# Recurrent branch of a two-layer hybrid block: preparation, solve and chunk chain laid out anew, TensorE in program order inside the branch

## The chip, the cores and the metric

One core of a Trainium2 chip runs the whole program: two layers of a diffusion-transformer block on one sequence, the second layer with a mixture of experts. The metric is the device time of one execution in microseconds. Before the change three executions took 2982.87, 2986.39 and 2990.86 us; the median is 2986.39 us.

## What is computed

Each layer projects the normalised tokens (256 context tokens and 256 tokens of the sequence, 512 together) into the inputs of three branches: latent attention, neighbourhood attention and a recurrent branch in the manner of RWKV-7. The branches are gated, merged and added to the tokens, and a feed-forward part follows, dense in layer 0, with experts in layer 1. Only the recurrent branch matters here. Its reference is a scan over tokens with a 64x64 state per head, 8 heads, once forward and once backward, over the context first and then over the sequence:

```
def step(S, inp):
    r_t, w_t, k_t, v_t, kk_t, a_t = inp
    sa = jnp.einsum('bhij,bhj->bhi', S, -kk_t)
    S = S * w_t[:, :, None, :] + sa[..., None] * (kk_t * a_t)[:, :, None, :] + v_t[..., None] * k_t[:, :, None, :]
    return S, jnp.einsum('bhij,bhj->bhi', S, r_t)
```

Before the scan, `kk` is the key times a gain, normalised to length 1 per head; the decay is w = exp(-exp(w_log)), with w_log from a low-rank projection of tanh; `a` is a sigmoid of a low-rank projection; the direction's key is k(1 + (a - 1) k_a). After it the two directions are added, normalised per head, a bonus (the sum over a head of r, the keys and a gain, times v) is added, and the whole is gated.

## The kernel before

**Layout.** The projections are computed transposed: a tile is 128 channels by 512 tokens. Four such tiles hold the 512 channels of r, k and v each. The branch takes them in two halves (f = 0 and 1) of two tiles, that is four heads; `rw_half` (L587) does one half, in these stages.

**Front** (`rw_front`, L551). For both tiles: kk times its gain, its square on ScalarE, the sum of squares per head by a matmul with a 0/1 matrix (L562), square root, maximum and reciprocal on 64 x 512 elements (L565 to L568), a matmul that spreads the result over each head's channels (L572), and the product. Then v is transposed (L581). In the first half the front runs first; in the second it is a generator that the chain of the first half advances step by step, from its fourth step on.

**Preparation** (L600 to L665). For each tile i and direction d: two low-rank matmuls (L609, L614), two tanh on ScalarE, an affine line (L618), a scan that sums the logarithms of the decay within chunks of 64 tokens (L620), for the backward direction two lines that turn the sum around (L622, L623), the exponentials P and iP (L626, L627), the decay over a whole chunk PC (L632), and the scaled operands: KR from kk and r (L635 to L641), BK from iP, a, and the direction's key (L644 to L653). Temporaries share one tag with five buffers (L548). At the end of each tile i stands the bonus: a VectorE line (L660), a matmul with a block matrix (L662) and the product with v (L664).

**Solve and merge.** Small pair matmuls inside the chunks (L684, L686), masked by VectorE (L689); VectorE transposes (L697), solves triangular systems of 16 x 16 in 14 steps of two lines (L703, L705) and transposes back (L709, L710). TensorE then builds the inverses of 32 and of 64 from them with 32 x 32 matmuls: L719, L735 and L739, L763 and L764, L771 and L772, with copies between them by VectorE and ScalarE.

**Chain** (L876 to L912). Eight steps, each of which takes one chunk forward and one backward. A step multiplies the old state with KR (L882), copies the right side (ScalarE, L885), applies the inverse (L892), copies the result (VectorE L894, ScalarE L895), adds to the state (L847, then the product with the decay on VectorE, L850) and writes outputs (L858, L865). The next step's inner products, masks, transposed keys and right side are computed in between (`inner`, `mask`, `keys`, `right`).

**Output** (`rw_out`, L918). Mean and variance per head on VectorE, transposes (L938), gain, bonus, gate (L943) and the store.

**What sets the order.** The program's text gives every engine an order of priority; the planner of the framework then lists the instructions of each engine, and takes an instruction of lower priority first where by its cost model the earlier one isn't ready. The rest of TensorE's work in this stage is the filler: `serve` (L451) yields the input projections tile by tile, each in 8 steps of three matmuls (a weight is split into a high and a low part, L314 to L316; ScalarE makes the high part, L469, and GpSimd the low part, L470), and after each tile it advances the modulation of a later stage (L339). `weave` (L1634) runs the stages' generators and draws filler from `serve`, as much as their yields ask for, in microseconds of TensorE time; a table of numbers per layer gives the yields (L1691):

```
K.W = (dict(prep=5.517, solve=1.0, merge=2.541, chain=1.41, front=1.212, mod=0.976), ...)[l]
weave(rwkv(l, t0), K.srv, False)
```

There is a yield behind each preparation (L658), several in the solve (L696 to L711), two in front of L735 and L763, two in the merge and three in each step of the chain. What is left of the filler goes to the attention that follows (L1700). In layer 1 the tiles which are needed for the sequence alone have 256 columns. `need` (L497) draws filler until a given tile is there; `shift` (L503) makes the branch's inputs of a finished tile, one line on ScalarE and two on VectorE. PSUM has five banks for the branch, two for the projections and one for the modulation.

Of the kernel before, what the change touches and what calls it, by code (L numbers as in the profile page):

```python
# [14 lines left out]
AF = mybir.ActivationFunctionType  # L15
OP = mybir.AluOpType
# [8 lines left out]
DEC = math.exp(-0.5)  # L25
# [160 lines left out]
class Kern:  # L186
# [346 lines left out]
    def rw_common(s, l):  # L533
        nc = s.nc
        s.rw_derived(l)
        s.share()
        for tag, n in (("z", 6), ("kk", 2), ("lora", 1), ("kds", 1)):
            s.t([128, T], tag, n)
        s.g2 = s.t([128, 512], "g2", 1)
        nc.sync.dma_start(s.g2, s.I["lora"][l, :, 2])  # L540
        s.m16 = s.t([128, 96], "m16", 1)
        nc.sync.dma_start(s.m16, s.I["cst"][:, KCST:])
        s.wd = s.need("wd")
        nc.scalar.activation(s.wd, s.wd, AF.Tanh)
        s.ad = s.need("ad")
# [5 lines left out]
    def rw_front(s, l, f, t0y):  # L551

        V, A, PE = s.nc.vector, s.nc.scalar, s.nc.tensor
# [3 lines left out]
        for i in range(2):  # L557
            q = s.t([128, T], "kk", 2)
            V.tensor_scalar(q, k[i], s.col(l, "kk", 2 * f + i), None, op0=OP.mult)
            sq = s.tmp()  # L560
            A.activation(sq, q, AF.Square)
            PE.matmul(st[32 * i:32 * i + 32], s.c("hs")[:, 2:], sq, start=True, stop=True)  # L562
            kk.append(q)
        rt = s.tmp()
        A.activation(rt[:64], st[:64], AF.Sqrt)  # L565
        yield 1.0
        V.tensor_scalar(rt[:64], rt[:64], 1e-12, None, op0=OP.max)
        V.reciprocal(rt[:64], rt[:64])  # L568
        yield 3.0
        for i in range(2):  # L570
            p = s.ps(tag="rw")
            PE.matmul(p, s.c("hst", 128)[32 * i:32 * i + 32], rt[32 * i:32 * i + 32], start=True, stop=True)  # L572
            V.tensor_tensor(kk[i], kk[i], p, OP.mult)
# [13 lines left out]
    def rw_half(s, l, f, t0y):  # L587
# [14 lines left out]
        for i in range(2):  # L602
            hp = 2 * f + i
            kd0 = None
            for d in range(2):
# [12 lines left out]
                V.tensor_scalar(lw, lw, -0.5 * DEC, -0.5 * DEC, op0=OP.mult, op1=OP.add)  # L618
                cum = s.tmp()
                V.tensor_tensor_scan(cum, s.c("scanm"), lw, 0.0, OP.mult, OP.add)  # L620
                if d:
                    V.tensor_tensor(lw, lw, cum, OP.subtract)  # L622
                    V.tensor_tensor(c8(lw), c8(lw), c8(cum)[:, :, 63:64].to_broadcast([128, 8, 64]), OP.add)  # L623
                    cum = lw
                P, iP = s.tmp(), s.tmp()
                A.activation(P, cum, AF.Exp)  # L626
                A.activation(iP, cum, AF.Exp, scale=-1.0)  # L627
                P8, q8 = c8(P), c8(kk[i])
                e = 0 if d else 63
                for a in (0, 4):  # L630
                    P4 = P8[:, a:a + 4, e:e + 1]
                    V.tensor_tensor(PC[:, a:a + 4, i, d], (P4[:, ::-1] if d else P4).to_broadcast([128, 4, 2]),  # L632
                                    s.c("hs")[:, 2:4].unsqueeze(1).to_broadcast([128, 4, 2]), OP.mult)
# [9 lines left out]
                u = s.tmp()  # L643
# [5 lines left out]
                kd = s.t([128, T], "kds", 1) if not d else s.tmp()  # L649
                V.tensor_scalar(kd, ta, s.kc2[l][:, hp:hp + 1], s.kc1[l][:, hp:hp + 1], op0=OP.mult, op1=OP.add)  # L650
                V.tensor_tensor(kd, kd, k[i], OP.mult)
# [7 lines left out]
            u = s.tmp()  # L659
            V.scalar_tensor_tensor(u[:, t0y:], kd0[:, t0y:], s.col(l, "rk", hp), r[i][:, t0y:], op0=OP.mult, op1=OP.mult)  # L660
            pb = s.ps(tag="rw")
            PE.matmul(pb[:, t0y:], s.c("bd"), u[:, t0y:], start=True, stop=True)  # L662
            bn = s.t([128, T], "bonus", 2)
            V.tensor_tensor(bn[:, t0y:], pb[:, t0y:], v[i][:, t0y:], OP.mult)  # L664
# [46 lines left out]
        yield s.W["solve"] * 4.0  # L711
# [11 lines left out]
        yield s.W["solve"] * 2.0  # L723
# [31 lines left out]
        yield s.W["solve"] * 3.0  # L755

        W = s.piece(2, 2048, 32, 32)
        for j in range(2):
            p = s.ps(tag="rw")
# [6 lines left out]
            V.tensor_copy(W[64:96, 16 * j:16 * j + 16, :].rearrange("p a b -> p (a b)"), p[64:96])  # L766
            p = s.ps(tag="rw")
# [5 lines left out]
            yield s.W["merge"]  # L773
# [93 lines left out]
        st = {}  # L867
# [8 lines left out]
        for n in range(8):  # L876
# [12 lines left out]
            yield s.W["chain"]  # L889
# [6 lines left out]
            yield s.W["chain"]  # L896
            if not last:
                mask(n + 1, 0, nx)
                Hn = end(n, H, st)
                mask(n + 1, 1, nx)  # L900
                values(n + 1, nx)
            if out:
                outputs(n, H, st)
            if not last:
                keys(n + 1, nx)
                right(n + 1, nx)
                H, st = Hn, nx
            yield s.W["chain"]
# [9 lines left out]
    def rw_out(s, l, f, R, t0):  # L918
# [14 lines left out]
        V.tensor_tensor(y, y, st[:, 2, :g].unsqueeze(2).to_broadcast([128, g, 64]), OP.mult)  # L933
        for i in range(2):
# [711 lines left out]
def body(tc, I, O, dbg=None, marks=None):  # L1646
    with ExitStack() as ctx:
# [9 lines left out]
        def rwkv(l, t0):  # L1657
            K.rw_common(l)
            for f in range(2):
# [4 lines left out]
                K.rw_out(l, f, K.R, t0)  # L1664
                yield 1.0

        for l in range(2):
            t0 = 256 * l
            with K.phase(f"o{l}", True, mm=2, md=1):
# [20 lines left out]
                with K.phase(f"rw{l}", rw=5):  # L1690
                    K.W = (dict(prep=5.517, solve=1.0, merge=2.541, chain=1.41, front=1.212, mod=0.976), dict(prep=4.665, solve=1.0, merge=2.178, chain=1.56, front=1.173, mod=0.666))[l]  # L1691
                    weave(rwkv(l, t0), K.srv, False)
# [62 lines left out]
```

## Time and profile before

| what | value |
|---|---|
| median of three runs | 2986.39 us |
| the profiled execution's own time | 2989.12 us |
| its span in the profile | 2987.4 us |
| mean granted clock of TensorE | 0.957 of full |
| busy: TensorE, VectorE, ScalarE, GpSimd | 2815.1, 1901.3, 1621.5, 369.9 us |
| HBM read and written | 554.38 and 24.64 MB |

A row of the waits says which instruction waited for which, in total, how often and the longest. Lines are those of the kernel above; `prw` is a PSUM bank of the branch, `pmm` one of the projections. "issue" is time in which the engine waited for nothing that the profile shows. In a view by stretches each engine's busy time is followed by the number of its instructions in brackets; the granted clock is a share of full speed, whose two levels are 1.0 (2.4 GHz) and 0.5 (1.2 GHz). A matmul on f32 data appears as several records.

### The profile page before, as it was taken

How to read it: one execution, taken by the hardware profiler on the slowest of the kernel's cores; microseconds unless marked ns; L12 is line 12 of the kernel's file. 1: busy time of each engine (PE TensorE's matmuls, PEld its weight loads, DVE VectorE, ACT ScalarE, POOL GpSimd, SP SyncE). 2: the span in 40 equal slices, each digit the busy share in tenths (PEclk: the TensorE clock that was granted, in tenths of full speed). 3: DMA queues.
4: the chain of work that ended last, by engine and by line, in shares of the span. 5: the costliest groups of instructions: out<-in, count | busy, mean ns of one | idle time of the engine just before them, and what ended most of it. 6: DMA issues, size and time to landing. Idle time of an engine off the chain costs nothing. (4 is left out here: it accounts for less than half of the span.)

```text
span 2987.4 us, 48726 instructions
## 1 busy us (share of the span) xinstructions
PE 2815.1 (94%) x19774; PEld 2168.4 (73%) x19774; DVE 1901.3 (64%) x2654; ACT 1621.5 (54%) x2449; POOL 369.9 (12%) x287
## 2 busy tenths in 40 slices
PE   7989979999999999997997979989999999999998
PEld 3566667676777888765766856778878787887876
DVE  4653662527754333267347256779988988888897
ACT  3423423447644332253343436667877777777776
POOL 3221221220010000133233400010000000000000
PEclk9989979999999999998997988989999999999999
DMA  7433311441432333343342333669989999998995
GB/s 273 160 130 103 131 57 61 158 143 57 128 127 80 97 99 104 117 143 110 103 149 95 108 104 109 193 239 361 359 320 363 353 350 342 356 361 335 362 352 205
DMA packets 109016, 582.26 MB, mean 195 GB/s; under 512 B 12912, under 2 KB 26608, under 8 KB 86896
## 3 DMA queue, kind: packets, MB, share of 16 engines
q1 hardware_dynamic: 94640, 557.57, 52.1%
q10 hardware_dynamic: 13632, 19.93, 1.8%
q8 instruction: 157, 2.57, 0.4%
q0 software_dynamic: 512, 1.57, 0.1%
q14 instruction: 75, 0.61, 0.1%
HBM read 554.38 MB, written 24.64 MB: 194 GB/s over the span
## 5 line engine op out<-in xcount | busy, mean ns | idle before, releaser
L314 PE MATMUL pmm<-big,whi 128*128 128x512 f32 (+2 forms) x1392 | 534.4, 385 | 11.1 <-ACT stage L958 3.2
L315 PE MATMUL pmm<-big,whi 128*128 128x512 f32 (+2 forms) x1392 | 517.4, 372 | 7.3 <-DVE big L436 3.6
L316 PE MATMUL pmm<-big,wlo 128*128 128x512 f32 (+2 forms) x1392 | 515.9, 371 | 1.9 <-POOL wlo L470 1.9
L1552 DVE TENSOR_TENSOR mwlo<-share,mwhi 128x1024 fp32r<-128x1024 f32 x398 | 472.2, 1229 | 21.0 <-ACT mwhi L1551 11.7
L1551 ACT ACTIVATE mwhi<-share 128x1024 fp32r<-128x1024 f32 x404 | 423.8, 1059 | 94.2 <-PE pmm L316 68.2
L470 POOL TENSOR_TENSOR wlo<-wraw,whi 128x512 fp32r<-128x512 f32 (+1 forms) x228 | 305.0, 1341 | 721.5 <-ACT whi L469 691.9
L315 PE MATMUL pmm<-mwlo,big 128*128 128x512 f32 x896 | 355.1, 396 | 7.2 <-DVE mwlo L1552 6.7
L314 PEld LDWEIGHTS pmm<-big,whi 128*128 128x128 f32 (+1 forms) x1392 | 267.4, 192 | 117.5 <-issue 37.5
L314 PE MATMUL pmm<-mwhi,big 128*128 128x512 f32 x896 | 352.1, 393 | 0.6 <-ACT big L1439 0.6
L316 PE MATMUL pmm<-mwhi,big 128*128 128x512 f32 x896 | 349.8, 390 | 0.0
L299 DVE TENSOR_TENSOR wlo<-wraw,whi 128x512 fp32r<-128x512 f32 x236 | 158.7, 674 | 252.1 <-ACT whi L298 245.6
L1552 DVE TENSOR_TENSOR mwlo<-mraw,mwhi 128x1024 fp32r<-128x1024 f32 x264 | 310.9, 1223 | 9.1 <-ACT mwhi L1551 3.5
L1551 ACT ACTIVATE mwhi<-mraw 128x1024 fp32r<-128x1024 f32 x264 | 278.0, 1060 | 66.8 <-PE pmm L316 49.8
L315 PEld LDWEIGHTS pmm<-big,whi 128*128 128x128 f32 (+1 forms) x1392 | 267.9, 192 | 55.1 <-DVE big L436 6.0
L316 PEld LDWEIGHTS pmm<-big,wlo 128*128 128x128 f32 (+1 forms) x1392 | 268.1, 193 | 50.6 <-issue 5.1
L298 ACT ACTIVATE whi<-wraw 128x512 fp32r<-128x512 f32 x236 | 145.3, 617 | 288.4 <-PE pmm L315 271.9
L469 ACT ACTIVATE whi<-wraw 128x512 fp32r<-128x512 f32 (+1 forms) x228 | 141.8, 624 | 267.4 <-PE pmm L315 228.3
L315 PEld LDWEIGHTS pmm<-mwlo,big 128*128 128x128 f32 x896 | 168.3, 188 | 48.0 <-DVE mwlo L1552 12.3
L314 PEld LDWEIGHTS pmm<-mwhi,big 128*128 128x128 f32 x896 | 168.3, 188 | 36.3 <-ACT big L1439 1.3
L316 PEld LDWEIGHTS pmm<-mwhi,big 128*128 128x128 f32 x896 | 168.3, 188 | 33.4
L315 PE MATMUL pat<-mwlo,mhh 128*128 128x512 f32 x448 | 175.1, 391 | 1.6 <-DVE mwlo L1552 1.4
L314 PE MATMUL pat<-mwhi,mhh 128*128 128x512 f32 x448 | 174.4, 389 | 0.0
(407 smaller groups left out, 4487.0 us busy)
## 6 DMA issues: line engine op xcount, KB each, us to landing
share<-in_moe SPq DMA_DIRECT2D x100, 2048.0 KB, 9.4
mraw<-in_moe SPq DMA_DIRECT2D x66, 2048.0 KB, 9.5
wraw<-in_win SPq DMA_DIRECT2D x112, 512.0 KB, 3.5
wraw<-in_modw SPq DMA_DIRECT2D x80, 512.0 KB, 4.9
wraw<-in_ffn SPq DMA_DIRECT2D x60, 512.0 KB, 3.5
wraw<-in_wo SPq DMA_DIRECT2D x24, 512.0 KB, 3.8
wraw<-in_wout SPq DMA_DIRECT2D x16, 512.0 KB, 4.6
share<-in_modw SPq DMA_DIRECT2D x12, 512.0 KB, 9.0
```

Of the source, the lines that this page charges most:

```text
L298: nc.scalar.activation(hi, raw[:, a:a + b], AF.Copy)
L299: nc.vector.tensor_tensor(lo, raw[:, a:a + b], hi.bitcast(F32), OP.subtract)
L314: nc.tensor.matmul(out, a[0], b[0], start=first, stop=False)
L315: nc.tensor.matmul(out, a[0], b[1], start=False, stop=False)
L316: nc.tensor.matmul(out, a[1], b[0], start=False, stop=last)
L469: nc.scalar.activation(hi, raw[:, k:k + 4], AF.Copy)
L470: nc.gpsimd.tensor_tensor(lo, raw[:, k:k + 4], hi.bitcast(F32), OP.subtract)
L1551: nc.scalar.activation(hi, raw[:, a:a + 2], AF.Copy)
L1552: (nc.gpsimd if a in pool else nc.vector).tensor_tensor(lo, raw[:, a:a + 2], hi.bitcast(F32), OP.subtract)
```

## The change

- Front: the sums of squares come out with tokens on partitions (8 matmuls with 2 columns), so root, maximum and reciprocal work on 128 x 16 elements; 16 matmuls with a broadcast operand spread them again.
- Preparation: both affine lines go to ScalarE, where one takes its constant from a column added to `m16`; the backward scan runs over reversed views, and L622 and L623 fall away; P, u and the backward key reuse buffers; the forward PC is one line in place of two; the key's lines stand earlier.
- Bonus: VectorE's line writes into the bonus tile; matmul and product with v move into the chain's first two steps.
- Yields: solve 8 in place of 4 ahead of L719, none in front of L735 and L763, one in the merge, between its two first groups, one per chain step in place of three, one ahead of the output's transposes; new numbers in the table. In a chain step the masks and keys of the next step stand earlier.
- Order: the branch runs inside `manual_schedule` for TensorE, so TensorE's instructions of the branch, filler drawn in it included, are issued in program order. The other engines keep the planner's order.

```diff
@@ -538,8 +538,9 @@
-    s.m16 = s.t([128, 96], "m16", 1)
-    nc.sync.dma_start(s.m16, s.I["cst"][:, KCST:])
+    s.m16 = s.t([128, 97], "m16", 1)
+    nc.sync.dma_start(s.m16[:, 0:96], s.I["cst"][:, KCST:])
+    nc.vector.memset(s.m16[:, 96:97], -0.5 * DEC)
@@ -559,17 +561,23 @@
-        PE.matmul(st[32 * i:32 * i + 32], s.c("hs")[:, 2:], sq, start=True, stop=True)
+        for tt in range(4):
+            o = 8 * i + 2 * tt
+            PE.matmul(st[:, o:o + 2], sq[:, 128 * tt:128 * tt + 128], s.c("hs")[:, 2:4], start=(o == 0), stop=True,
+                      skip_group_check=True)
...
-    rt = s.tmp()
-    A.activation(rt[:64], st[:64], AF.Sqrt)
-    yield 1.0
-    V.tensor_scalar(rt[:64], rt[:64], 1e-12, None, op0=OP.max)
-    V.reciprocal(rt[:64], rt[:64])
-    yield 3.0
+    rt = s.t([128, 16], "rt", 2)
+    A.activation(rt, st[:, 0:16], AF.Sqrt)
+    V.tensor_scalar(rt, rt, 1e-12, None, op0=OP.max)
+    V.reciprocal(rt, rt)
+    yield 1.5
...
-        PE.matmul(p, s.c("hst", 128)[32 * i:32 * i + 32], rt[32 * i:32 * i + 32], start=True, stop=True)
+        for tt in range(4):
+            o = 8 * i + 2 * tt
+            for hh in range(2):
+                PE.matmul(p[64 * hh:64 * hh + 64, 128 * tt:128 * tt + 128], rt[:, o + hh:o + hh + 1].to_broadcast([128, 64]), s.id,
+                          start=(tt == 0), stop=True, skip_group_check=True)
@@ -615,22 +623,22 @@
-            V.tensor_scalar(lw, lw, -0.5 * DEC, -0.5 * DEC, op0=OP.mult, op1=OP.add)
+            A.activation(lw, lw, AF.Identity, bias=s.m16[:, 96:97], scale=-0.5 * DEC)
...
-            V.tensor_tensor_scan(cum, s.c("scanm"), lw, 0.0, OP.mult, OP.add)
-            if d:
-                V.tensor_tensor(lw, lw, cum, OP.subtract)
-                V.tensor_tensor(c8(lw), c8(lw), c8(cum)[:, :, 63:64].to_broadcast([128, 8, 64]), OP.add)
-                cum = lw
-            P, iP = s.tmp(), s.tmp()
+            rev = (lambda a: a[:, ::-1]) if d else (lambda a: a)
+            V.tensor_tensor_scan(rev(cum), s.c("scanm"), rev(lw), 0.0, OP.mult, OP.add)
+            P, iP = lw, s.tmp()
...
+            kd = s.t([128, T], "kds", 1) if not d else cum
+            A.activation(kd, ta, AF.Identity, bias=s.kc1[l][:, hp:hp + 1], scale=s.kc2[l][:, hp:hp + 1])
+            V.tensor_tensor(kd, kd, k[i], OP.mult)
...
-            for a in (0, 4):
-                P4 = P8[:, a:a + 4, e:e + 1]
-                V.tensor_tensor(PC[:, a:a + 4, i, d], (P4[:, ::-1] if d else P4).to_broadcast([128, 4, 2]),
-                                s.c("hs")[:, 2:4].unsqueeze(1).to_broadcast([128, 4, 2]), OP.mult)
+            for a, b in ((0, 4), (4, 8)) if d else ((0, 8),):
+                P4 = P8[:, a:b, e:e + 1]
+                V.tensor_tensor(PC[:, a:b, i, d], (P4[:, ::-1] if d else P4).to_broadcast([128, b - a, 2]),
+                                s.c("hs")[:, 2:4].unsqueeze(1).to_broadcast([128, b - a, 2]), OP.mult)
@@ -640,15 +648,12 @@
-            u = s.tmp()
+            u = P
...
-            kd = s.t([128, T], "kds", 1) if not d else s.tmp()
-            V.tensor_scalar(kd, ta, s.kc2[l][:, hp:hp + 1], s.kc1[l][:, hp:hp + 1], op0=OP.mult, op1=OP.add)
-            V.tensor_tensor(kd, kd, k[i], OP.mult)
@@ -656,12 +661,8 @@
-        u = s.tmp()
-        V.scalar_tensor_tensor(u[:, t0y:], kd0[:, t0y:], s.col(l, "rk", hp), r[i][:, t0y:], op0=OP.mult, op1=OP.mult)
-        pb = s.ps(tag="rw")
-        PE.matmul(pb[:, t0y:], s.c("bd"), u[:, t0y:], start=True, stop=True)
...
-        V.tensor_tensor(bn[:, t0y:], pb[:, t0y:], v[i][:, t0y:], OP.mult)
+        V.scalar_tensor_tensor(bn[:, t0y:], kd0[:, t0y:], s.col(l, "rk", hp), r[i][:, t0y:], op0=OP.mult, op1=OP.mult)
@@ -708,7 +709,7 @@
-    yield s.W["solve"] * 4.0
+    yield s.W["solve"] * 8.0
@@ -720,7 +721,6 @@
-    yield s.W["solve"] * 2.0
@@ -752,10 +752,11 @@
-    yield s.W["solve"] * 3.0
...
+        if j:
+            yield s.W["merge"]
@@ -764,13 +765,13 @@
+    for j in range(2):
...
-        yield s.W["merge"]
@@ -886,26 +887,30 @@
         if not last:
             inner(n + 1, nx)
         begin(n, H, st, out)
-        yield s.W["chain"]
+        if not last:
+            mask(n + 1, 0, nx)
         pu = [s.ps(tag="rw") for _ in range(2)]
         for i, hh, d, q in heads:
             PE.matmul(pu[d][bp(n, d), 64 * q:64 * q + 64], TT[HO[d], 16 * hh + 8 * i + ch[d], :], Rs[HO[d], 64 * q:64 * q + 64],
                       start=(q == 0), stop=(q == 3), skip_group_check=True)
         V.tensor_copy(st["uv"][0][bp(n, 0)].rearrange("p a b -> p (a b)"), pu[0][bp(n, 0), 0:256])
         A.activation(st["uv"][1][bp(n, 1)].rearrange("p a b -> p (a b)"), pu[1][bp(n, 1), 0:256], AF.Copy)
-        yield s.W["chain"]
         if not last:
-            mask(n + 1, 0, nx)
+            mask(n + 1, 1, nx)
+            keys(n + 1, nx)
+        yield s.W["chain"][f]
+        if not last:
             Hn = end(n, H, st)
-            mask(n + 1, 1, nx)
             values(n + 1, nx)
         if out:
             outputs(n, H, st)
         if not last:
-            keys(n + 1, nx)
             right(n + 1, nx)
             H, st = Hn, nx
-        yield s.W["chain"]
+        if n < 2:
+            pb = s.ps(tag="rw")
+            PE.matmul(pb[:, t0y:], s.c("bd"), bonus[n][:, t0y:], start=True, stop=True)
+            V.tensor_tensor(bonus[n][:, t0y:], pb[:, t0y:], v[n][:, t0y:], OP.mult)
         if n > 2:
             w = next(front, None)
             if w:
@@ -931,6 +936,7 @@
+    yield s.W["out"]
@@ -1661,8 +1667,7 @@
-            K.rw_out(l, f, K.R, t0)
-            yield 1.0
+            yield from K.rw_out(l, f, K.R, t0)
@@ -1688,8 +1693,10 @@
-                K.W = (dict(prep=5.517, solve=1.0, merge=2.541, chain=1.41, front=1.212, mod=0.976), dict(prep=4.665, solve=1.0, merge=2.178, chain=1.56, front=1.173, mod=0.666))[l]
-                weave(rwkv(l, t0), K.srv, False)
+                K.W = (dict(prep=5.5, solve=1.1, merge=1.9, chain=(1.9, 1.2), front=1.2, out=5.0, mod=0.976),
+                       dict(prep=4.7, solve=1.1, merge=1.9, chain=(1.9, 1.2), front=1.2, out=5.0, mod=0.666))[l]
+                with tc.manual_schedule(engines={mybir.EngineType.PE}):
+                    weave(rwkv(l, t0), K.srv, False)
```

## Rows read from the trace of the kernel before

**Rows 1.** Part 2 of the page: the span in 40 slices, in tenths.

```profile
PE   7989979999999999997997979989999999999998
...
PEclk9989979999999999998997988989999999999999
```

**Rows 2.** TensorE's waits, layer 0's recurrent branch: total us, times, longest us.

```profile
PE prw L662 <- DVE t L660: 16.2, 4, 6.7
PE prw L735 <- issue: 7.0, 4, 2.0
PE prw L719 <- DVE share L709: 6.8, 1, 6.8
```

**Rows 3.** TensorE's waits in the recurrent branch of layer 1.

```profile
PE prw L719 <- DVE share L709: 14.2, 2, 8.7
PE prw L662 <- DVE t L660: 12.9, 4, 4.2
PE prw L938 <- DVE share L933: 6.7, 2, 5.9
```

**Rows 4.** Stretches of layer 0: stretch, length, busy by engine, granted clock, DMA.

```profile
105.70:156.70 51.00, 44.58 (x170) 24.37 (x170) 39.45 (x59) 18.67 (x31) 12.43 (x9) 0.92 0.46 151
...
338.40:388.60 50.20, 40.33 (x149) 26.13 (x152) 42.67 (x61) 19.20 (x33) 16.03 (x12) 0.89 0.27 95
...
395.30:416.90 21.60, 14.83 (x62) 11.87 (x61) 20.40 (x33) 5.00 (x9) 6.70 (x5) 0.90 0.30 97
416.90:448.10 31.20, 25.84 (x928) 21.47 (x928) 9.85 (x13) 7.41 (x13) 4.44 (x4) 0.70 0.05 18
448.10:534.00 85.90, 85.90 (x949) 64.55 (x949) 21.41 (x39) 30.41 (x64) 16.35 (x13) 1.00 0.24 83
```

**Rows 5.** The same view, three stretches of layer 1.

```profile
1326.20:1370.60 44.40, 37.98 (x172) 23.54 (x171) 37.98 (x57) 19.77 (x34) 18.15 (x12) 0.96 0.51 164
...
1544.20:1592.50 48.30, 38.85 (x188) 26.21 (x187) 41.46 (x61) 19.77 (x35) 20.49 (x14) 0.86 0.42 143
...
1599.10:1623.00 23.90, 15.21 (x117) 15.01 (x119) 22.66 (x33) 7.92 (x16) 12.12 (x9) 0.79 0.37 116
```

**Rows 6.** VectorE by line, layer 0, second half: xcount, busy us, mean ns, idle before.

```profile
L651 DVE TENSOR_TENSOR t<-t,z 128x512 f32<-128x512 f32 x2 | 3.5, 1757 | 0.0
L618 DVE TENSOR_SCALAR t<-t 128x512 f32<-128x512 f32 x4 | 2.8, 694 | 2.0 <-ACT t L612 2.0
...
L664 DVE TENSOR_TENSOR bonus<-prw,z 128x512 f32<-128x512 f32 x2 | 1.4, 692 | 4.3 <-PE prw L662 4.3
...
L653 DVE TENSOR_TENSOR share<-kds,t 128x512 f32<-128x512 f32 x2 | 1.4, 680 | 0.0
```

**Rows 7.** TensorE in order of time, first preparation: start us, duration us.

```profile
105.68 1.12 PE L609 MATMUL prw<-zl,lora 64*128 64x512 f32 x2
...
120.94 1.07 PE L339 MATMUL pmd<-wraw,sT 128*32 128x512 f32 x8
```

**Rows 8.** One step of the chunk chain in order of time: start us, duration us.

```profile
485.50 0.40 PE L315 MATMUL pmm<-big,whi 128*128 128x512 f32 x1
...
485.73 0.39 PE L316 MATMUL pmm<-big,wlo 128*128 128x512 f32 x1
...
487.42 0.68 PE L892 MATMUL prw<-rs,share 64*64 64x64 f32 x16
...
488.13 0.42 DVE L894 COPY uv<-prw 64x256 f32<-64x256 f32 x1 [2.61 <-PE prw L892]
...
490.40 0.69 DVE L850 TENSOR_TENSOR hst<-prw,pc 128x512 f32<-128x512 f32 x1 [1.84 <-PE prw L847]
```

**Rows 9.** GpSimd by line, the stretch of group 6.

```profile
L470 POOL TENSOR_TENSOR wlo<-wraw,whi 128x512 fp32r<-128x512 f32 x11 | 16.1, 1468 | 29.0 <-ACT whi L469 29.0
```

**Rows 10.** What follows the branch: layer 0's stretch and layer 1's, as group 4.

```profile
546.00:700.00 154.00, 147.17 (x714) 107.02 (x712) 73.23 (x128) 84.54 (x162) 37.53 (x30) 0.98 0.39 128
1745.00:1900.00 155.00, 140.74 (x788) 93.08 (x789) 108.62 (x250) 93.05 (x200) 1.42 (x3) 0.84 0.34 109
```

## The prediction

> **What bounds the kernel now.** I read the page first: TensorE is nearly always busy, and where its busy tenths fall its granted clock falls with them: behind the start in the slices at 150, 373, 1344, 1568 and 1718 us, each 74.7 us long [rows 1]. The first four lie in the recurrent branches of the two layers, two halves in each, the only stage that the change touches; the fifth lies where layer 1's branch ends. There I read TensorE's waits. Three of them carry a cost: L662, the bonus matmul at the end of a preparation, waits for VectorE 16.2 us in layer 0 and 12.9 us in layer 1; L719, the first matmul behind the triangular solve, waits 6.8 and 14.2 us; L938 waits 6.7 us in layer 1 [rows 2, 3]. Then the stretches. Each preparation (from L609 to L684) lasts 51.0, 50.2, 44.4 and 48.3 us with VectorE busy for 38 to 43 of them. The chunk chain is the contrary: TensorE is busy for all of its 85.9 us, at full clock [rows 4, 5]. So preparation and solve are VectorE's, the chain is TensorE's, and all the rest of TensorE's time is projection matmuls ("filler"), which are the same in number after the change. Less filler in one stage is no gain, since it is done later; gained are TensorE's waits and its time at the lower clock. I therefore sum by stage, against the profiled run's own 2989.1 us.
>
> **Preparation, four stretches.** VectorE loses six groups: both affine lines (L618, L650 twice), L622 and L623 (a reversed scan replaces them) and L664 (to the chain). From L618 to L664 they sum to 2.8 + 2.2 + 2.0 + 1.4 + 1.1 + 1.4 = 10.9 us of the 42.7 us busy in that stretch [rows 4, 6]. The stretch also holds the output's last lines and a modulation, by my estimate 3.8 us, so 28 us remain. The reversed scan is not in the trace: at best it costs what the forward one does, at worst that and the two lines which it replaces (2.2 + 1.4 us for two backward directions, 1.8 each). I take the forward price, since the same 512 elements pass. To these come the head (one matmul, then tanh, and now one more ScalarE line ahead of the scan) and two waits for the exponentials, by estimate 2.5 and 1.5 us. VectorE thus needs 32 us, and 37.5 if the collisions below all stay. TensorE in program order issues L609 and its like L614 four times, 1.1 us each, 8.5 in all, and four portions of filler. A filler matmul takes 0.23 us from start to start, so one tile of 24 takes 5.5 us, and with each tile comes a modulation group of 1.07 us [rows 7, 8]. Counting the yields, layer 0 gets 22.4 us nominal, that is 4.4 tiles: 24 + 4.5 + 8.5 = 37 us. Layer 1, with a smaller portion and some narrower tiles, comes to 31 us. The longer of the two sides counts: 37 us in layer 0, 34 in layer 1. Savings are 14 + 13 + 10 + 14 = 51, less 1 for the tails: **+50**. Bounds: TensorE alone gives 59, VectorE at 37.5 and 1 us of tail 40.
>
> One row speaks for the worse bound. L651's backward form takes 1757 ns where L653, with the same shape, takes 680 [rows 6]; 11 GpSimd subtractions, 1468 ns each, run in that stretch [rows 9]. The Trainium skill (SBUF — State Buffer, section Who interferes with whom) says that a VectorE instruction with two SBUF inputs contends with a GpSimd instruction that reads SBUF, and that whichever issues first makes the other wait. By that rule moving L618 and L650 to ScalarE takes away collisions but not subtractions, all 11 would strike the lines that remain at 1.08 us each, and the sum would have +40 in place of +50.
>
> **Solve and merge.** After L684 the program gives TensorE 21.8 us nominal of filler ahead of L719, before it was 15.4 to 16.0. At 0.23 us a matmul that is 23 us of matmuls, with modulation 25 to 27; VectorE's solve stretch is 21.6 to 23.9 us [rows 4, 5]. So the L719 waits go: +21.0 (6.8 + 14.2). In return no filler stands between L719, L735 and L763. The small matmuls there wait for "issue", 7.0 us in 4 waits [rows 2]; eight places lose their filler, and if one wait of 1.75 us came up in each it would be 14, I take half: -7, bounds 0 and -14. The filler that stood there ran at a granted clock of 0.70 [rows 4]; 10 us of it in each half moves to better places, at most 4 us each, I take 6 in all. At the start of the chain the masks and the first copy have nothing to hide them: 1 us per half, -4. Together **+16**, bounds 0 and +30.
>
> **Chain.** Three portions of filler per step become one. TensorE was never idle there, so leaving filler out moves it and no more. Added: the bonus matmul, twice in each half, 1.1 us in layer 0 as L609's pair of the same 512 columns [rows 7], 0.6 us in layer 1 with half of them: **-7**. The waits that lose cover: L894 starts at 488.13, as L892 ends at 488.10, and takes 0.42 us; L850 follows L847 and takes 0.69 us [rows 8]. A group of 16 small matmuls takes 0.68 us there, and by that price the transposes with 1.2 or 1.9 us of filler stand before L847, the output and right-hand groups (1.4 us) before the next L882, only the latter in the first four steps of layer 1. I take **-2**; bare hand-overs are the rival below.
>
> **Front, output, seams.** The norm's matmuls shrink and its broadcasts grow from 2 to 16 small ones, about nothing (+1 to -2 us a half), and the reciprocal over 512 columns was under filler. But in order TensorE now stands at the last squares and the v transposes, since they wait for tiles just finished: a shift (two lines of VectorE), the scaling, the square, by estimate 3.5 us less a modulation group and three filler matmuls (1.75 us) that follow the tile, **-4** over both layers. L938 gets 5.1 us nominal of filler in front of it: layer 1 gains 5.9 of its 6.7 us [rows 3]; layer 0, where no filler may now be pulled forward and twice as many tokens are normalised, loses about 3 us per half: **0**. Other seams (the second L684 group, which waits for the end of the preparation): 1.5 us per half, **-6**.
>
> **Attention of layer 1.** By the yields the branch used up all of layer 1's filler before; now 41 us nominal are left for the stretch behind it. That stretch is busy for 140.7 of 155 us at a clock of 0.84; layer 0's, which has filler, for 147.2 of 154 at 0.98 [rows 10]. Equal idleness gives 7.5 us. Equal clock is worth 0.14 x 155 = 22 us where TensorE sets the pace; I count a quarter: **+13**, bounds 0 and +29.
>
> Sum: 50 + 16 - 7 - 2 - 4 + 0 - 6 + 13 = 60. 2989.1 - 60 = 2929; the median of the runs shown stands 2.7 us lower, so **2926 us**.
>
> **Rivals.**
> A, slower: the fixed order bares the hand-overs. Before, a waiting step let the planner put filler in front; now everything behind the waiting instruction on TensorE waits, filler too. Each chain step (four chains of 8, worth 31 steps, as each last one lacks a hand-over) has three hand-overs of about 0.9 us (copy 0.4 to 0.7 and the way there and back). If ScalarE's conversions and VectorE's shifts stand in front of the copies, all three lie bare at 2.7 us, 84 us: 2926 + 84 = 3010. It decides from 60/31 = 1.9 us per step. For it: filler per step falls to a third. Against it: of the 85.9 us some 36 are filler by the yields, so each of 8 steps keeps 6.2 us of its own matmuls, nearly half of them between L882 and L892.
> B, near no change: VectorE still ends each preparation, L684 waits where L662 did (40 in place of 50), the seams cost 6 us per half in place of 1.5, and each drops the clock as L662's waits do now (0.86 to 0.92 in three of the four preparations [rows 4, 5]), some 3 us per half. 10 + 18 + 12 = 40 is lost, and attention's 13 don't come: 2979.
> C, better: TensorE-bound preparation (+59), solve and merge +30, attention +29: 2926 - 9 - 14 - 16 = 2887.
> That TensorE's order hardly changes is a fourth way, but it would alter nothing in the yields and so ends near the forecast.
>
> **How the numbers follow.** Forecast 0.62, its own range 2905 to 2955; C 0.10; B 0.17; A 0.11. The range 2888 to 2978 takes in C and most of B and leaves out A. A change can be told from none above 0.3%, 9 us: faster is the forecast, C and half of B, 0.80; the same is the other half of B and a weak form of A, 0.10; slower is the rest of A, 0.10.
>
> **What would show it.** Right: no wait of 3 us or more at the bonus matmul or at the first matmul behind the solve, preparations of 34 to 37 us, no reciprocal of 3.3 us, chains that are shorter by their filler with TensorE over 95% busy, projection matmuls between the attention matmuls of layer 1. Wrong: waits on the chain's copies of over 1.9 us per step (A), preparations of 40 us and more with a wait at the small pair matmuls (B), or a stretch after layer 1's branch as idle as now.

## The result and the profile after

The changed kernel takes 2937.07 us (median of 4 runs, 2935.88 to 2949.78), the kernel before, beside it, 2988.24: ratio 0.9841, 95% interval [0.981, 0.9871]. The forecast was 2926, within 2888 to 2978. The profiled run took 2937.55 us, span 2935.8. The direction holds and the sum is 11 us off; the experiments show that two of the reasons don't hold.

Lines move a little: L609 is now L617, L684 and L686 are L685 and L687, L719 is L720, L789 is L790, L850 is L851, L858 is L859, L938 is L944, and the bonus matmul L662 is L912 in the chain.

Part 2 of the page of the changed kernel, as [rows 1]:

```profile
PE   6989989999999999988998999899999999999998
...
PEclk9989989999999999999797999989999999999999
```

TensorE's waits in layer 0's branch of the changed kernel (total us, times, longest), as [rows 2]:

```profile
PE prw L859 <- DVE hst L851: 11.2, 14, 1.0
PE prw L735 <- issue: 7.2, 4, 2.8
PE prw L687 <- issue: 5.4, 2, 2.9
...
PE prw L944 <- DVE share L938: 1.7, 2, 1.4
PE pmd L347 <- ACT stage L344: 1.5, 1, 1.5
```

The same in layer 1's branch, as [rows 3]:

```profile
PE prw L735 <- issue: 6.4, 4, 2.6
PE prw L685 <- issue: 5.7, 2, 3.4
PE prw L859 <- DVE hst L851: 4.7, 6, 0.8
PE prw L720 <- issue: 4.5, 2, 3.1
PE pmm L314 <- DVE z L512: 3.4, 1, 3.4
PE pmd L347 <- ACT stage L344: 2.5, 1, 2.5
```

The three waits that carried a cost are gone or small: no VectorE wait at the bonus matmul or behind the solve, 1.7 us where L938 waited. New ones are L859's, 15.9 us over both layers, and "issue" waits in the pair matmuls, 11.1 us.

Stretches of the changed kernel (length, busy by engine, granted clock, DMA), as [rows 4, 5, 10]: preparation, merge, preparation, merge, chain with normalisation; layer 1's two preparations; the stretch behind its branch:

```profile
109.80:146.70 36.90, 36.90 (x158) 21.33 (x158) 28.78 (x42) 23.37 (x39) 11.56 (x8) 1.00 0.51 167
...
186.00:214.90 28.90, 21.14 (x914) 17.20 (x913) 9.45 (x14) 7.28 (x13) 3.75 (x4) 0.65 0.18 59
...
313.40:349.90 36.50, 36.50 (x151) 21.78 (x150) 29.06 (x40) 22.03 (x36) 12.33 (x10) 1.00 0.61 202
386.70:413.20 26.50, 19.59 (x908) 17.54 (x907) 7.46 (x11) 6.11 (x11) 3.16 (x3) 0.65 0.10 33
413.20:488.70 75.50, 69.72 (x891) 54.57 (x889) 30.55 (x49) 28.04 (x59) 7.65 (x6) 0.96 0.20 68
1314.10:1345.30 31.20, 31.20 (x142) 18.27 (x141) 26.73 (x39) 22.77 (x38) 10.97 (x8) 1.00 0.52 171
...
1500.90:1536.30 35.40, 33.53 (x179) 22.57 (x178) 29.81 (x39) 24.22 (x42) 19.04 (x13) 1.00 0.57 188
...
1670.30:1825.30 155.00, 146.25 (x997) 114.30 (x995) 98.60 (x212) 96.90 (x208) 42.94 (x34) 0.98 0.49 159
```

Preparations of 36.9, 36.5, 31.2 and 35.4 us, in three of them TensorE never idle. The two merges run at 0.65, that is at 1.2 GHz for about 70% of their time.

To compare stages that hold different amounts of filler I take off each stage its projection matmuls at 0.2275 us per 512 columns from start to start (an estimate; [rows 8] have 0.23) and its modulation, 1.07 us a group [rows 7]. What is left, summed over the four halves, before and after: preparation 86.5 and 39.2 us; pairs and solve 58.2 and 55.8; merge 94.8 and 101.4; chain with normalisation 212.3 and 222.5; the start of the branch +4.2; everything behind layer 1's branch 570.6 and 548.3. Below, "net" is this figure. It comes from the one profiled run of each kernel, and e1's (2894.08 us) lies 14 us under its median, those of e2 and e9 7 under theirs and e12's 4 above, so nets are compared by stage and not by their sum.

### The profile page after: what moved, and what is told of

It reads as the page before. It is cut to its first block, busy times and chain, and to the rows that moved or that the text cites. A ratio compares the mean times of both kernels' runs of the same rounds, so it can differ in the third digit from the quotient of the medians.

```text
span 2935.8 us, 49055 instructions
## 1 busy us (share of the span) xinstructions
PE 2779.2 (95%) x19934; PEld 2178.8 (74%) x19934; DVE 1859.8 (63%) x2600; ACT 1636.8 (56%) x2479; POOL 370.9 (13%) x287
## 5 line engine op out<-in xcount | busy, mean ns | idle before, releaser
L314 PE MATMUL pmm<-big,whi 128*128 128x512 f32 (+2 forms) x1392 | 535.7, 385 | 13.0 <-DVE z L512 3.4
L316 PE MATMUL pmm<-big,wlo 128*128 128x512 f32 (+2 forms) x1392 | 519.0, 373 | 4.6 <-POOL wlo L470 4.6
L1558 DVE TENSOR_TENSOR mwlo<-share,mwhi 128x1024 fp32r<-128x1024 f32 x398 | 472.0, 1226 | 21.1 <-ACT mwhi L1557 11.7
L314 PEld LDWEIGHTS pmm<-big,whi 128*128 128x128 f32 (+1 forms) x1392 | 271.7, 195 | 115.2 <-issue 29.8
L314 PE MATMUL pmm<-mwhi,big 128*128 128x512 f32 x896 | 352.5, 394 | 0.6 <-ACT big L1445 0.6
L316 PE MATMUL pmm<-mwhi,big 128*128 128x512 f32 x896 | 350.4, 391 | 0.0
L1557 ACT ACTIVATE mwhi<-mraw 128x1024 fp32r<-128x1024 f32 x264 | 277.9, 1060 | 68.4 <-PE pmm L316 51.6
L315 PEld LDWEIGHTS pmm<-big,whi 128*128 128x128 f32 (+1 forms) x1392 | 271.6, 195 | 53.6 <-DVE big L436 6.3
L316 PEld LDWEIGHTS pmm<-big,wlo 128*128 128x128 f32 (+1 forms) x1392 | 271.2, 195 | 51.7 <-POOL wlo L470 6.5
L314 PEld LDWEIGHTS pmm<-mwhi,big 128*128 128x128 f32 x896 | 168.5, 188 | 36.4 <-ACT big L1445 1.3
L316 PEld LDWEIGHTS pmm<-mwhi,big 128*128 128x128 f32 x896 | 168.6, 188 | 33.4
L314 PE MATMUL pat<-mwhi,mhh 128*128 128x512 f32 x448 | 174.5, 389 | 0.0
```

What stands on the lines that cost most here:

```text
L314: nc.tensor.matmul(out, a[0], b[0], start=first, stop=False)
L315: nc.tensor.matmul(out, a[0], b[1], start=False, stop=False)
L316: nc.tensor.matmul(out, a[1], b[0], start=False, stop=last)
L1557: nc.scalar.activation(hi, raw[:, a:a + 2], AF.Copy)
L1558: (nc.gpsimd if a in pool else nc.vector).tensor_tensor(lo, raw[:, a:a + 2], hi.bitcast(F32), OP.subtract)
```

## The experiments

Each ran four times (e4 ten times) beside the kernel before. Differences are taken between ratios, times 2988. The front's new form, the reused buffers and the earlier masks and keys were not run alone.

| run | us | ratio, 95% interval |
|---|---|---|
| changed | 2937.07 | 0.9841 [0.981, 0.9871] |
| e1 no order | 2908.45 | 0.9748 [0.9717, 0.9779] |
| e2 before + order | 3033.24 | 1.0164 [1.0133, 1.0195] |
| e3 old VectorE lines | 2947.65 | 0.9874 [0.9844, 0.9904] |
| e4 bonus back | 2967.74 | 0.9946 [0.9927, 0.9966] |
| e5 right first | 2921.90 | 0.9777 [0.976, 0.9793] |
| e6 before + bonus moved | 2948.54 | 0.9861 [0.9841, 0.9882] |
| e7 no order, bonus back | 2934.10 | 0.9825 [0.9803, 0.9848] |
| e8 no order, filler in pairs | 2899.68 | 0.9699 [0.9679, 0.9719] |
| e9 e8 + filler in merge | 2889.59 | 0.9677 [0.9661, 0.9693] |
| e10 no order, old portions | 2936.49 | 0.9832 [0.9816, 0.9849] |
| e11 order, e5 and e8's edits | 2910.05 | 0.9739 [0.9723, 0.9756] |
| e12 e9 + more in merge | 2873.18 | 0.9601 [0.9585, 0.9617] |

**The bonus matmul: e4, e6, e7.** e4 and e7 (e7 without program order) put it back at the end of each tile's preparation; e6 is the kernel before with this move alone.

```
+            pb = s.ps(tag="rw")
+            PE.matmul(pb[:, t0y:], s.c("bd"), bn[:, t0y:], start=True, stop=True)
+            V.tensor_tensor(bn[:, t0y:], pb[:, t0y:], v[i][:, t0y:], OP.mult)
...
-            if n < 2:
-                pb = s.ps(tag="rw")
-                PE.matmul(pb[:, t0y:], s.c("bd"), bonus[n][:, t0y:], ...)
```

> The bonus matmul and its product go back to the end of each tile's preparation, before the pairs. Theory: VectorE is quicker now, TensorE waits 2 to 4 us per half for the end of VectorE's work, and the preparation grows by 1 to 3 us a half, the chain loses 2 matmuls and 2 products a half: 5 to 10 us slower than the changed kernel, 2942 to 2947 us. Rival, moving the bonus made the gain: 25 us or more slower, 2962 us or more.

> The kernel before with one part of the change alone: the bonus matmul and its product leave the preparation for chain steps 0 and 1. Theory after the first four runs: TensorE's wait for the bonus product was what tied each preparation to VectorE, so this part alone brings most of the preparation's gain, which comes back in part at the solve, since VectorE still has its old lines and the yields are the old ones: 2950 to 2965 us, preparations of 36 to 42 us. Rival, the bonus costs much only under program order (as in the run with it put back): within 8 us of the kernel before.

> Changed kernel without program order, and with the bonus matmul back at the end of each tile's preparation. Theory, the bonus wait ties TensorE to VectorE whoever orders it: 20 us or more slower than the run without program order alone (2908), 2928 to 2945 us. Rival, the planner covers the wait with filler: at most 8 us slower, 2908 to 2916 us.

e4 costs 31 us, where I expected 5 to 10: the rival was right. e6 gains 41 us by itself, a little more than my range; e7 is 23 us slower than e1, as its theory had it. So the place of the matmul and its product decides, in the old layout and the new, with and without program order. The two moved together in all three runs; which of them holds the stage more was not separated. TensorE's waits in e4, layer 0 and then layer 1 (L667 is the matmul put back):

```profile
PE prw L667 <- DVE bonus L665: 10.4, 4, 3.0
...
PE prw L667 <- DVE bonus L665: 14.5, 4, 3.7
```

and e6, whose VectorE lines are the old ones but for the product, which moved along: the second preparation, and the largest waits of layer 0's branch:

```profile
331.10:359.70 28.60, 28.60 (x109) 18.95 (x108) 28.40 (x46) 14.78 (x25) 11.17 (x8) 1.00 0.33 111
```

```profile
PE prw L680 <- DVE share L646: 8.1, 2, 5.4
```

That preparation is 28.6 us long, with TensorE busy throughout, where before it took 50.2 [rows 4]; a part of that is less filler in it (109 matmul records for 149). The four take 36.8, 28.6, 30.9 and 34.6 us, net 42 in all for 86.5. What VectorE has not finished is found behind them, in front of the second pair group (L680): 13.0 us over both layers, where L662 had 29.1.

The gains do not add up. e7, with neither the move nor program order, is 52 us below the kernel before, net some 12 each in the preparations (86.5 to 75) and in pairs and solve and 22 behind layer 1's branch. The move alone gives 41, and both together, e1, 75: they share some 18 us, and what the move is worth, 23 to 41 us, depends on what else has been done.

**VectorE's lines: e3.** The affine lines and the turning of the backward sums go back to VectorE.

```
-                A.activation(lw, lw, AF.Identity, bias=s.m16[:, 96:97], scale=-0.5 * DEC)
+                V.tensor_scalar(lw, lw, -0.5 * DEC, -0.5 * DEC, op0=OP.mult, op1=OP.add)
...
+                if d:
+                    V.tensor_tensor(lw, lw, cum, OP.subtract)
+                    V.tensor_tensor(c8(lw), c8(lw), c8(cum)[:, :, 63:64]..., OP.add)
...
-                A.activation(kd, ta, AF.Identity, bias=..., scale=...)
+                V.tensor_scalar(kd, ta, ..., op0=OP.mult, op1=OP.add)
```

> The four affine lines of each half (two of each kind per tile and direction, 8 a half) go back from ScalarE to VectorE and the two turning lines of the backward direction with them; the bonus matmul stays in the chain. Theory: VectorE sets the preparation's length, so some 9.5 us of VectorE work a half come back, 38 us over four halves less what the preparation's remaining waits absorb: 2965 us (2955 to 2978), preparation 43 to 46 us a half. Rival, the bonus matmul's waiting at TensorE was all of it: no more than 8 us slower than the changed kernel, 2945 us or less.

It costs about 10 us, and the two intervals overlap; my theory asked for 28, the rival for 8 at most, which is nearer. The preparation stays as it was, and the lag appears at the second pair group, here L688. First preparation of e3, then its waits at L688 in layer 0 and in layer 1:

```profile
109.50:146.40 36.90, 36.90 (x155) 21.32 (x155) 32.18 (x50) 17.79 (x30) 9.67 (x8) 1.00 0.51 172
```

```profile
PE prw L688 <- DVE share L657: 6.6, 2, 4.1
...
PE prw L688 <- DVE share L657: 8.8, 2, 5.5
```

15.4 us of waits, of which the stage pairs and solve shows 12 (net 55.8 to 67.7). Together e3 and e4 say: of the preparation's gain the bonus move brings most, and once it is made the lighter VectorE brings some 10 us more, not inside the preparation. With the bonus in its old place (e7) the preparations did shrink under the new lines.

**Program order: e1, e2, e5, e11.** e1 takes one line out of the changed kernel, e2 puts it alone into the kernel before; e5 exchanges two calls in the chain.

```
-                    with tc.manual_schedule(engines={mybir.EngineType.PE}):
-                        weave(rwkv(l, t0), K.srv, False)
+                    weave(rwkv(l, t0), K.srv, False)
```
```
+            if not last:
+                right(n + 1, nx)
             if out:
                 outputs(n, H, st)
             if not last:
-                right(n + 1, nx)
                 H, st = Hn, nx
```

> Theory: the gain is made by the VectorE lines and the bonus product that left the preparation, which stay out here; without program order the planner may again pull filler into TensorE's waits, among them the waits of outputs() for end()'s multiplication (15.9 us in all) and the stalled transposes of the solve (some 10 us), and may again put pieces badly. About 2930 us, 2915 to 2950. Rival, TensorE's program order makes the gain: 2975 us or more, as without any gain in the solve and the preparation. What tells them apart is the length of the preparation (L617 to L685): 35 us a half by the theory, 44 or more by the rival.

> Theory: program order alone gains nothing in the preparation, where TensorE waits for VectorE, and takes from the old kernel the filler that its planner put into waits: 2980 to 3015 us, preparation 45 us or more a half. Rival, program order makes the gain: about 2945 us.

> In the changed kernel outputs() waits 0.78 us at L859 in each of 20 chain steps, 15.9 us in all, for end()'s multiplication L851, which reads the same PSUM tile. Here right(n + 1), 16 matmuls of 0.68 us which need neither, goes in front of outputs(). Theory, the wait is real and costs its length: 20 x 0.68 = 13.6 us less than the changed kernel (2937.07), 2923 us, L859's waits gone. Rival, the time comes back at the next waits (the copy of the right-hand sides, the masks): no change, 2935 to 2940 us.

> Changed kernel with program order, with right(n + 1) ahead of outputs(n) and the filler between the pair groups. It asks what program order still costs once its one large wait is gone. Theory, outputs() was the larger part and some 10 us of small waits remain (front, first merge matmuls): 2908 to 2915 us against 2899.7 without order. Rival, nothing remains: 2897 to 2904 us.

Order costs 28 us in the changed kernel (e1, better than my range); e1's preparations of 36.8, 35.3, 31.2 and 37.9 us rule out the rival that order makes the gain. It costs 49 us in the old kernel (e2, worse than my range; preparations of 47 to 54 us), there net 12 in the preparations, 10 in the merges and 21 in the chains, where L858 waits 15.7 us for L850, less 11 in pairs and solve. A chain step of the changed kernel in order of time (start, duration, idle before):

```profile
251.27 0.73 PE L848 MATMUL prw<-uv,bn 128*64 128x64 f32 x16
...
252.04 0.69 DVE L851 TENSOR_TENSOR hst<-prw,pc 128x512 f32<-128x512 f32 x1 [2.92 <-PE prw L848]
252.79 0.55 PEld L859 LDWEIGHTS prw<-uv,am 128*64 128x64 f32 x16 [0.92 <-DVE hst L851]
252.79 0.69 PE L859 MATMUL prw<-uv,am 128*64 128x64 f32 x16 [0.78 <-DVE hst L851]
```

and of e1:

```profile
242.68 0.73 PE L848 MATMUL prw<-uv,bn 128*64 128x64 f32 x16
...
243.34 0.68 PE L812 MATMUL prw<-share,am 64*64 64x64 f32 x16
243.45 0.69 DVE L851 TENSOR_TENSOR hst<-prw,pc 128x512 f32<-128x512 f32 x1 [2.93 <-PE prw L848]
243.95 0.74 PEld L566 LDWEIGHTS prw<-cst,t 128*128 128x128 f32 x6
```

outputs() (L859) uses other columns of the tile `ph` than L851 reads, and yet starts 0.06 us after L851's end. The Trainium skill (PSUM — Partial Sum Buffer, section PSUM bank collisions raise a hardware error) says that two engines must not access one bank within the same partitions at the same time, and that software has to guard by bank and by group of 32 partitions, not by address. The trace agrees in that the disjoint columns wait; which rule of the framework set this wait no run shows. The planner had put right() (L812) into the gap; the fixed order has nothing there. e5 does it by hand: L859's waits fall from 15.9 to 3.6 us, and 19 us are gained by the ratios, 15 by the medians, for 13.6 expected. In e11 12 us of order's price remain against e8, as expected; by net times they lie in the merge (102.4 for 93.5), in pairs and solve (43.9 for 36.1) and in the start of the branch, less 6 in the chain and 4 in the preparation. What costs the merge was not isolated.

**The filler portions: e10.** e1 with the old yields (three of 1.41 or 1.56 in each chain step, 4, 2 and 3 around the solve, none in front of the output).

```
-                    K.W = (dict(prep=5.5, solve=1.1, merge=1.9, chain=(1.9, 1.2), ...
+                    K.W = (dict(prep=5.517, solve=1.0, merge=2.541, chain=1.41, ...
```

> Changed kernel without program order and with the old places and sizes of the filler portions. Theory, the new distribution is what keeps filler for the stretch behind layer 1's branch (22 us there, L720 free of waits besides): 2908 + 22 + 5 = 2935 us (2928 to 2945), with that stretch's net time back from 548 to 570 us. Rival, the planner makes up for it: 2908 to 2918 us.

25 us by the ratios, 28 by the medians: the theory. The stretch behind layer 1's branch has its old idleness and clock again, 0.85 (0.84 in [rows 10], 0.98 in the changed kernel), and is net 567.4 us instead of 548.4 in e1. Merges, chains and pairs with solve are net some 9, 14 and 5 us longer as well, the preparations 7 shorter; this was not taken apart. The stretch:

```profile
1694.00:1849.00 155.00, 142.35 (x810) 95.52 (x809) 110.70 (x254) 95.27 (x206) 1.42 (x3) 0.85 0.34 114
```

**Waits for issue: e8, e9, e12.** All without program order. e8 puts a portion behind each of the first three pair groups in place of the 3.0 behind all; e9 adds 0.4 of a merge portion before L720's second block and before each block of L735 and L739; e12 two more. The chain's portions pay (1.9, 1.2, then 1.6, 0.9, then 1.4, 0.7).

```
+                if q < 3:
+                    yield s.W["solve"]
...
-        yield s.W["solve"] * 3.0
...
+            yield s.W["merge"] * 0.4
```

> Changed kernel without program order, and the 3.0 of filler that stood behind the pair matmuls is spread over the three gaps between their four groups of 32. It asks whether the waits for issue in the pair stage (2.8 + 2.9 + 3.6 + 1.7 = 11 us in the run without program order) come from many small matmuls in a row. Theory, they do: these waits go, 2898 us (8 to 12 us less than 2908). Rival, they come with the code's length and only change their place, or VectorE gets the pairs later and the solve ends later: 2905 to 2918 us.

> The run with filler between the pair groups, and three more small portions of filler (0.4 of a merge portion each) between the blocks of small matmuls from L720 to L739; the chain's portions shrink from 1.9 and 1.2 to 1.6 and 0.9 to pay for them. Theory, the waits for issue belong to many small matmuls in a row, so the 28 to 30 us of them that are left in solve and merge fall to about half: 2885 to 2893 us. Rival, filler put there runs at half clock, as the merge does (17 to 20 us a half at 0.50), and costs twice: 2900 to 2912 us.

> The run with filler between the merge's blocks, and two more portions (0.4 of a merge portion each): after L739's second block and before the last block of small matmuls, paid for by the chain's portions (1.4 and 0.7). Theory, issue waits and the half clock of the merge give way further: 2880 to 2886 us. Rival, the chain has too little filler left for its hand-overs, or the merge is at its limit: 2888 to 2900 us.

e8 gains 15 us by the ratios, 9 by the medians, as the theory had it, though its interval just touches e1's. The pairs' waits in e1, layer 0; in e8 none of 0.2 us or more is left there, and 0.5 us in layer 1:

```profile
PE prw L685 <- issue: 2.9, 1, 2.9
PE prw L687 <- issue: 2.8, 1, 2.8
```

A long row of small matmuls is not enough for these waits: the same pairs have 0.6 us of them in the kernel before and in e7 and none in e2 and e4, the four kernels in which TensorE has just stood at the bonus matmul.

e9 is 10 us below e8 by the medians, 7 by the ratios, with intervals that overlap, and inside its range; e12 is 16 below e9 by the medians, 23 by the ratios, better than its range. The theory holds in part. All issue waits in the four halves sum to 38.5 us in e1, 30.4 in e8, 23.0 in e9 and 18.0 in e12; half was expected of e9. The granted clock changes too. The first and the second merge in e8, in e9 and in e12:

```profile
176.70:203.60 26.90, 20.16 (x853) 16.28 (x852) 9.64 (x16) 7.73 (x14) 4.42 (x4) 0.62 0.17 56
368.60:393.90 25.30, 17.54 (x844) 15.66 (x843) 6.35 (x11) 5.51 (x10) 3.15 (x3) 0.66 0.11 35
```
```profile
177.60:204.50 26.90, 20.80 (x861) 16.04 (x860) 9.66 (x15) 8.73 (x16) 5.69 (x5) 0.81 0.19 66
366.90:390.50 23.60, 20.41 (x853) 16.89 (x853) 8.12 (x11) 5.11 (x9) 3.17 (x3) 0.71 0.06 19
```
```profile
177.50:204.90 27.40, 21.82 (x929) 16.29 (x928) 9.31 (x15) 9.28 (x16) 5.70 (x5) 0.88 0.28 94
367.50:395.80 28.30, 24.54 (x925) 19.62 (x925) 8.89 (x12) 6.82 (x12) 4.41 (x4) 0.76 0.09 32
```

The first merge keeps about its length with 3.0, 5.1 and 6.5 us of filler in it, and its granted clock rises from 0.62 to 0.88: with two levels, 2.4 GHz for about a quarter and then three quarters of the stretch. The second shows the limit: from e9 to e12 it grows by 4.7 us for 2 us of filler. All four merges last 102.6 us in e8 with 9 us of filler, 102.3 in e9 with 19 and 111.3 in e12 with 26 (net 93.5, 83.7 and 85.5). So the filler that e9 adds costs no time there, mostly because it takes the place of issue waits (7.5 of the 9.8 us net); what the clock gives beside them was not separated. In e12 the merges gain nothing more; by net times its gain on e9 lies in the chains (9 us less), whose portions shrank, which was not run alone. e12 is the best version, 4% below the kernel before.

## Why the prediction came out, step by step

- **What bounds the preparation: wrong; its length: right.** In layer 0 the length was taken from TensorE's own queue, 37 us, and came out at 36.9 and 36.5; in layer 1 I wrote 34, above both of its sides (31 and 32) and without a sum, and it came out at 31.2 and 35.4. The term +50 is 47.3 net. But I booked the gain to VectorE's 10.9 us of lines and gave the stage to VectorE. e3 leaves the length at 36.9 us in layer 0 with all those lines back but L664; e6 shortens it while taking only L664 away. What tied the stage to VectorE was L662: TensorE stood there 29 us in all, and VectorE in turn stood behind it, 4.3 us at L664 in the second half alone [rows 6]. One queued consumer bound two engines to each other; I had the wait in hand, and counted it as a symptom. (The bound of 59 is 58 by its own lengths, which moves C from 2887 to 2888.)
- **Rule and row on collisions.** The collisions stayed, as the worse bound had it. VectorE by line in the second preparation after:

```profile
L629 DVE TENSOR_TENSOR_SCAN t<-cst,t 128x512 f32<-128x512 f32 x4 | 4.9, 1225 | 4.5 <-ACT t L626 4.5
...
L658 DVE TENSOR_TENSOR share<-t,t 128x512 f32<-128x512 f32 x2 | 3.5, 1773 | 0.0
...
L635 DVE TENSOR_TENSOR t<-t,z 128x512 f32<-128x512 f32 x2 | 1.4, 688 | 0.0
```

  L658 still takes 1773 ns where L635 of the same shape takes 688; both instructions of its row ran beside a GpSimd subtraction for 1.2 us, those of L635's for 0.03 us at most. Of the stretch's 8 subtractions 7 stood beside a slowed VectorE line. They show no cost here because TensorE ended the stage, not because they were gone. The scan in both directions takes 1225 ns: the forward price was right.
- **Solve and merge +16 with the seams -6: wrong.** The two stages that hold both (pairs and solve, merge) give 2.4 - 6.6 = -4 for +10. L719's waits for VectorE, 21.0 us, went as forecast. Two steps failed. The first is the term for issue waits: -7 stood for the merge and nothing for the pairs, but in these stages they rise from 20.4 to 39.6 us, of which the pairs have 11.1, where I had put the seams' wait for VectorE. The second is that order would cost these stages nothing beyond the seams; rival A charged it to the chain alone. Without it (e1) they give 12.5 + 3.8 = 16 with the same issue waits, 38.5 us, and order costs them net 20 us there, 13 in e4 against e7 and 17 in e11 against e8. Stalled filler (L347, L314 and L316, in order behind a copy, a shift or a subtraction) is little of it: 9.3 us of such waits in the changed kernel, 7.2 in e1. In the second halves pairs and solve run at a granted clock of 0.86, in e1 at 0.95. What order costs the merge stays open.
- **Chain -9: size right (-10.2), reason half.** The copies for `uv` are covered, as argued. The bare hand-over is outputs() behind L851, 15.9 us, which I had counted only as filler that covers something else. It is rival A in small: 0.8 us at 20 places, not 2.7 at 31. TensorE is busy for 92% of layer 0's chain stretches, not over 95; layer 1's have 96 and 97%.
- **Front -4, output 0: right** (the start of the branch is 4.2 us longer; L944 waits 1.7 us, in layer 0 alone).
- **Attention +13: too small, 22 measured,** and e10, which loses 19 of them with the old portions, shows that the filler kept for it does it. The clock is 0.98, so the full price of it was due, not a quarter.

The net terms sum to 51 us and the profiled runs differ by 51.6, for 60 forecast: 14 too many in solve, merge and seams, 3 in the preparation and 1 in the chain, 9 too few in attention. That the sum came this near is in part luck, since these errors cancel.

## What to carry to other kernels

A consumer that waits for a slow engine should not stand in an in-order queue ahead of the work that feeds that engine: busy shares of 80% on both sides may be one such tie, and moving the consumer was worth more here (23 to 41 us) than lightening the slow engine after it (about 10). If an order is fixed by hand, go through every pair of neighbours that share a PSUM bank with another engine's read, and put independent work between them. Leave filler for the stretches of small matmuls, in small portions: in e8 and e9 it took the place of issue waits there and cost no time; in e12 a further portion no longer shortened the merges.

## What the runs showed of the hardware that was not expected

- In long rows of small matmuls TensorE idles for "issue" (up to 3.6 us at a time and 38.5 us over four halves in e1, some 1100 records of small matmuls in each), and a few 512-column matmuls between the groups of 32 take the waits in the pairs away (11.1 us to 0.5, e8). Where TensorE has waited just ahead (the kernel before, e2, e4, e7) the pairs have at most 0.6 us of them. That the instructions come too late is a reading of this; no run shows it.
- In the first merge the clock is at 1.2 GHz for about 70% of the time although TensorE is busy for 21.1 of 28.9 us. With 4 to 5 us of filler spread through each merge the four run at 0.71 to 0.81 (e9), with 6 to 7 us at 0.71 to 0.94 (e12), and with 2 to 3 us in one place at 0.62 to 0.67 (e8). Whether amount or spread does it was not separated.
- The scan through a reversed view costs what the forward one does, 1225 ns.
